# Two mixers of a decoder trunk: float32r parts instead of float32 matmuls, the mask and the pooling sums on VectorE

## The chip, the cores and the metric

One NeuronCore of a Trainium2 chip runs the whole program. The metric is the device time of one execution in microseconds; the reference's outputs are computed in float32 from float32 inputs.

## What is computed

A trunk of two residual layers over 256 positions of width 1024. Each layer is SwiGLU (half step), a mixer, SwiGLU (half step), each behind an RMSNorm whose shift, scale and gate come from a conditioning vector. The even layer's mixer is causal pooling beside differential attention; the odd layer's is an mLSTM. What the change touches:

```python
def pool_mixer(u, w_group, scale):
    ...
    for g, w in enumerate(POOL_WINDOWS):                  # 2, 4, 8, 16
        csg = cs[:, :, g]                                 # cumulative sum over positions
        cs_pad = jnp.pad(csg, ((0, 0), (w, 0), (0, 0)))
        total = cs_pad[:, w:] - cs_pad[:, :S]
        count = jnp.minimum(pos + 1, w).astype(jnp.float32)
        means.append(total / count[None, :, None])
    pooled = jnp.stack(means, axis=2) - ug
    y = jnp.einsum('bsgc,gcd->bsgd', pooled, w_group.astype(jnp.float32))
    ...
def diff_attention(q, k, v, lam_params, subln_g, lambda_init):
    ...
        s = jnp.einsum('bqhcd,bkhcd->bhcqk', qblk, kf)
        s = jnp.where(key_pos[None, :] <= qpos[:, None], s, -jnp.inf)
        p = jax.nn.softmax(s, axis=-1)
        a = p[:, :, 0] - lam * p[:, :, 1]
...
def mlstm_chunkwise(q, k, v, i_pre, f_pre):
    ...
    m_t = jnp.maximum(inter_log, jnp.max(D, axis=-1))
    Dw = jnp.exp(D - m_t[..., None])
```

## The kernel before

Activations lie with features on the 128 partitions and the 256 positions along the free axis. Every weight matrix is cut into units of 128x128; `weight_units` lists them in the order in which they are used, and the host packs them so, 16 units to a DMA. `split_to` makes two float32r parts of each half chunk (8 units): ACT writes the high part `wh` (L297), DVE the low part `wl` (L298). `mm3` then takes a unit with three matmuls (L339 to L341): high by high, low by high, high by low. `unit` counts units, and 8 of them make a block of 128 output rows.

The rest of a mixer runs in generators, the lanes: `tick` goes through them at every unit, and a lane's `yield n` puts off its next piece by n units. `run_until` drives all lanes on at once where the result of one is needed. The compiler's scheduler orders each engine's instructions afterwards, so pieces move by a few matmuls.

Even mixer: `in_proj` computes 16 blocks in the order `EVEN_IN_ORDER` (q, k, v of each of four heads, then u3 to u0). DVE takes each out of PSUM (`ti`, L587), `done` keeps it (ACT, `keep`, L597) and starts lanes. `head` computes the scores of its two halves, on partitions 0 to 63 and 64 to 127: a float32r matmul of an identity with the mask (L624), then float32 matmuls into the same accumulation, 128 columns for the first 128 positions (L626), 256 for the others (L628). DVE takes the row maximum (L635), ACT the exponentials (L639). `pool_group` multiplies u with the group's `w_pool` (L694) and the result with a band matrix that holds mean minus identity (L699 to L701), all in float32; `split_y` (L571, L572) makes the parts of a result for the out projection. That runs over the eight results `ys` in the order `EVEN_OUT_K`, three output blocks side by side at first (`sweep(..., 3, 2)`), and `residual` adds each block to x and prepares the next norm (L436, L383, L384).

Odd mixer: `gates` forms per head the row of running maxima `mr` on 4 partitions and spreads it over 128 with a float32 matmul (L806), one per head, a yield of 6 between them.

`constants` builds masks and band matrices on POOL during the first FFN, in which DVE also sums the conditioning's products (`mod_sums`, L265); that work goes on through most of the run.

## Time and profile before

| | before |
|---|---|
| median of 3 runs | 1001.04 us (1000.83 to 1001.37) |
| profiled execution | 1001.05 us |
| its span, first to last instruction | 999.3 us |
| mean granted TensorE clock | 0.996 |
| PE busy | 980.7 us, 98% |
| DVE busy | 780.8 us, 78% |
| ACT busy | 523.5 us, 52% |
| POOL busy | 209.4 us, 21% |

Busy times are shares of the whole span, and the stages differ. Records of neighbouring instructions on PE overlap (a matmul's record is 0.28 us long and the next one starts 0.12 us later), so the distance of starts tells more than a record's length. A float32 matmul leaves two records, a float32r one or a transpose one. The even mixer runs from about 217 to 306 us, the odd one from about 690 to 800.

### The profile page before, as it was taken

What the parts mean: (1) busy time and instruction counts of PE and PEld (TensorE: products, weight loads), DVE (VectorE), ACT (ScalarE), POOL (GpSimd) and SP (SyncE); (2) the same over time, 40 slices, a digit from 0 to 9 for tenths busy, and PEclk for the clock granted to TensorE, in tenths of its full rate; (3) what the DMA queues carried; (4) which work ended last, traced back from release to release, by engine and by line L of the source; (5) the groups of instructions that cost most, each with busy time, mean ns of one, the idle gap of its engine ahead of it and who ended that gap; (6) DMA issues with size and microseconds to landing.
All of it is one profiled execution on the core that took longest, in us unless ns stands there. A gap on an engine that the chain in (4) does not pass through costs nothing.

```text
span 999.3 us, 19657 instructions
## 1 busy us (share of the span) xinstructions
PE 980.7 (98%) x8032; PEld 965.4 (97%) x8032; DVE 780.8 (78%) x1251; ACT 523.5 (52%) x832; POOL 209.4 (21%) x223
## 2 busy tenths in 40 slices
PE   7999999999999999999999999999999999999996
PEld 6899999998999999999999999999999999999996
DVE  5979998988879888877788888787768987777452
ACT  3475444446765545544454555444667655455441
POOL 4953220110012222211122222000010122222011
PEclk9999999999999999999999999999999999999998
DMA  8978888877647766766766766777546665554521
GB/s 341 318 293 320 328 328 319 343 287 261 216 157 262 257 251 251 258 258 243 285 228 246 264 250 250 268 283 288 212 173 216 255 237 214 205 217 176 187 103 43
DMA packets 36093, 247.18 MB, mean 247 GB/s; under 512 B 4001, under 2 KB 4385, under 8 KB 7458
## 3 DMA queue, kind: packets, MB, share of 16 engines
q1 hardware_dynamic: 35856, 245.81, 66.8%
q8 instruction: 63, 1.03, 0.4%
q14 instruction: 28, 0.23, 0.1%
q10 hardware_dynamic: 146, 0.11, 0.0%
HBM read 244.86 MB, written 1.05 MB: 246 GB/s over the span
## 4 chain that ended last, share of the span: by engine, by line
PE 79%; DVE 11%; ACT 4%; issue 4%; POOL 1%; DVEq 0%; ACTq 0%; POOLq 0%
PE one L339 26%; PE one L341 26%; PE one L340 25%; DVE wl L298 4%; DVE rawm L265 3%; ACT wh L297 2%; DVE xl L384 1%; POOL hr L393 1%; PE one L410 0%; DVE xa L436 0%; DVE acol L360 0%; DVE xl L557 0%; PE one L628 0%; DVE ti L587 0%; PE one L626 0%
## 5 line engine op out<-in xcount | busy, mean ns | idle before, releaser
L339 PE MATMUL one<-xh,wh 128*128 128x258 f32 (+1 forms) x1728 | 486.1, 286 | 1.9 <-ACT xh L555 1.9
L340 PE MATMUL one<-xh,wl 128*128 128x258 f32 (+1 forms) x1728 | 482.2, 283 | 2.1 <-DVE wl L298 2.0
L297 ACT ACTIVATE wh<-raww 128x1024 fp32r<-128x1024 f32 x320 | 337.9, 1058 | 277.2 <-PE one L341 247.5
L341 PE MATMUL one<-xl,wh 128*128 128x258 f32 (+1 forms) x1728 | 481.7, 283 | 0.2
L298 DVE TENSOR_TENSOR wl<-raww,wh 128x1024 fp32r<-128x1024 f32 x320 | 394.9, 1236 | 107.5 <-ACT wh L297 102.4
L339 PEld LDWEIGHTS one<-xh,wh 128*128 128x128 f32 x1728 | 325.7, 190 | 5.3 <-ACT xh L555 2.4
L340 PEld LDWEIGHTS one<-xh,wl 128*128 128x128 f32 x1728 | 326.0, 190 | 4.3 <-DVE wl L298 4.0
L341 PEld LDWEIGHTS one<-xl,wh 128*128 128x128 f32 x1728 | 322.7, 189 | 0.9 <-DVE xl L384 0.6
L339 PE MATMUL one<-hid,wh 128*128 128x256 f32 x832 | 233.8, 281 | 0.2 <-ACT hid L571 0.2
L341 PE MATMUL one<-hid,wh 128*128 128x256 f32 x832 | 233.7, 281 | 0.0
L340 PE MATMUL one<-hid,wl 128*128 128x256 f32 x832 | 233.3, 280 | 0.0
L468 POOL TENSOR_TENSOR hid<-h,hid 128x256 fp32r<-128x256 f32 x88 | 116.2, 1322 | 349.6 <-ACT hid L467 344.0
L339 PEld LDWEIGHTS one<-hid,wh 128*128 128x128 f32 x832 | 156.7, 188 | 0.4 <-ACT hid L571 0.4
L340 PEld LDWEIGHTS one<-hid,wl 128*128 128x128 f32 x832 | 156.8, 188 | 0.0
L341 PEld LDWEIGHTS one<-hid,wh 128*128 128x128 f32 x832 | 156.5, 188 | 0.2 <-DVE hid L572 0.2
L265 DVE CUSTOM_DVE_ANT_0 rawm<-rawm,cact,pk 128x1024 f32<-128x1024 f32 x112 | 150.5, 1370 | 0.0
L377 POOL TENSOR_TENSOR acc<-acc,sq 128x256 f32<-128x256 f32 x41 | 34.4, 839 | 272.0 <-ACT sq L373 271.8
L482 DVE TENSOR_TENSOR t<-one,rext 128x258 f32<-128x258 f32 x132 | 55.3, 422 | 31.1 <-PE one L341 30.2
L463 ACT ACTIVATE sg<-t 128x256 f32<-128x256 f32 x66 | 32.8, 500 | 33.7 <-DVE t L482 33.7
L467 ACT ACTIVATE hid<-h 128x256 fp32r<-128x256 f32 x88 | 36.8, 418 | 19.1 <-DVE h L465 18.7
L265 DVE CUSTOM_DVE_ANT_0 rawm<-rawm,cact,ghalf 128x1024 f32<-128x1024 f32 x32 | 44.8, 1428 | 0.0
L465 DVE SCALAR_TENSOR_TENSOR h<-t,sg 128x256 f32<-128x256 f32 x66 | 32.5, 492 | 8.4 <-ACT sg L463 0.6
(213 smaller groups left out, 503.7 us busy)
## 6 DMA issues: line engine op xcount, KB each, us to landing
raww<-wst SPq DMA_DIRECT2D x152, 1024.0 KB, 4.9
rawm<-mst SPq DMA_DIRECT2D x71, 1024.0 KB, 4.8
raww<-wst SPq DMA_DIRECT2D x16, 512.0 KB, 5.4
xa<-xT SPq DMA_DIRECT2D x2, 512.0 KB, 4.7
rawm<-mst SPq DMA_DIRECT2D x2, 512.0 KB, 7.2
outT<-fin SPq DMA_DIRECT2D x3, 256.0 KB, 2.8
pk<-pack SPq DMA_DIRECT2D x1, 416.0 KB, 6.3
outT<-fin SPq DMA_DIRECT2D x2, 128.0 KB, 2.3
```

The lines of the kernel that those rows point to most:

```text
L265: nc.vector.tensor_tensor_reduce(out=ri, in0=ri, in1=cact, scale=factor, scalar=first, op0=ALU.mult, op1=ALU.add, accum_out=modc[n // KT][ ...
L297: nc.scalar.activation(whs[i], src, AF.Copy)
L298: ins = nc.vector.tensor_tensor(out=wls[i], in0=src, in1=whs[i].bitcast(F32), op=ALU.subtract)
L339: nc.tensor.matmul(out, lhsT=wh, rhs=rh, start=start, stop=False, skip_group_check=skip)
L340: nc.tensor.matmul(out, lhsT=wl, rhs=rh, start=False, stop=False, skip_group_check=skip)
L341: nc.tensor.matmul(out, lhsT=wh, rhs=rl, start=False, stop=stop, skip_group_check=skip)
L377: eng.tensor_tensor(out=stat["acc"], in0=stat["acc"], in1=sq, op=ALU.add)
L463: nc.scalar.activation(sg, gate, AF.Silu, bias=bias_g)
L465: nc.vector.scalar_tensor_tensor(out=h, in0=up, scalar=bias_u, in1=sg, op0=ALU.add, op1=ALU.mult)
L467: nc.scalar.activation(hh[:, 0:T], h, AF.Copy)
L468: nc.gpsimd.tensor_tensor(out=hl[:, 0:T], in0=h, in1=hh[:, 0:T].bitcast(F32), op=ALU.subtract)
L482: nc.vector.tensor_tensor(out=t[:, i, :], in0=ts.pop((f, i))[:, 0:XC], in1=rext, op=ALU.mult)
```

## The change

- **Scores.** q and k are kept as two float32r parts (ACT the high, DVE the low one). A head's scores are twelve float32r matmuls instead of two mask matmuls and four float32 ones: for each of the two column ranges high by high, low by high, high by low, alternating between the halves on partitions 0 to 63 and 64 to 127. The mask is added by DVE in the operation that takes the maximum; it writes the masked scores to SBUF, from where ACT takes the exponentials. The lane waits 10 units instead of 8.
- **Pooling.** The sums over 2, 4, 8, 16 positions come first, by shifted additions on DVE, doubling each time; mean minus token goes into two float32r parts, and three matmuls of 256 columns with the parts of `w_pool` (made once on POOL) follow. The band matrices are gone; `icnt` holds 1/(t+1) for the first 16 positions.
- **Out projection.** `EVEN_OUT_K` takes the last head last, and four blocks run side by side at first, the last three of the eight results late; the host's packing follows.
- **Odd mixer.** `mr` is split into two float32r parts; each row is spread by two float32r matmuls.

```diff
-EVEN_OUT_K = (4, 5, 6, 3, 2, 7, 1, 0)
+EVEN_OUT_K = (4, 5, 6, 3, 2, 1, 0, 7)
+PAD = 16
...
         def head(h):
-            yield 8
+            yield 10
...
-            for c in range(2):
-                rows = slice(64 * c, 64 * c + 64)
-                nc.tensor.matmul(pp[c][:, 0:3 * P], lhsT=identr, rhs=masks3, start=True, stop=False,
-                                 skip_group_check=True)
-                nc.tensor.matmul(pp[c][:, 0:P], lhsT=q[rows, 0:P], rhs=kk[rows, 0:P], start=False, stop=True,
-                                 skip_group_check=True)
-                nc.tensor.matmul(pp[c][:, P:3 * P], lhsT=q[rows, P:T], rhs=kk[rows, 0:T], start=False, stop=True,
-                                 skip_group_check=True)
+            for to, qs, ks in ((slice(0, P), slice(0, P), slice(0, P)), (slice(P, 3 * P), slice(P, T), slice(0, T))):
+                for j, (a, b) in enumerate(((0, 0), (1, 0), (0, 1))):
+                    for c in range(2):
+                        rows = slice(64 * c, 64 * c + 64)
+                        nc.tensor.matmul(pp[c][:, to], lhsT=q[a][rows, qs], rhs=kk[b][rows, ks], start=j == 0,
+                                         stop=j == 2, skip_group_check=True)
...
-                    nc.vector.tensor_reduce(out=mx[:, i, c:c + 1], in_=pp[c][:, cols[i]], axis=AX.X, op=ALU.max)
+                    nc.vector.tensor_tensor_reduce(
+                        out=sc[:, c, cols[i]], in0=pp[c][:, cols[i]], in1=masks3[:, cols[i]], scale=1.0, scalar=NEG,
+                        op0=ALU.add, op1=ALU.max, accum_out=mx[:, i, c:c + 1])
...
         def pool_group(g, src, bias):
...
+            s, d = u, 1
+            while d < w:
+                n = tmp.tile([P, PAD + T], F32, tag="ps", name=nm("ps"))
+                lo = 2 * d - 1
+                nc.vector.tensor_tensor(out=n[:, lo:PAD + T], in0=s[:, lo:PAD + T], in1=s[:, lo - d:PAD + T - d],
+                                        op=ALU.add)
+                s, d = n, 2 * d
             z = slot()
...
+            nc.vector.scalar_tensor_tensor(out=z[:, 0:T], in0=s[:, PAD:PAD + T], scalar=1.0 / w,
+                                           in1=u[:, PAD:PAD + T], op0=ALU.mult, op1=ALU.subtract)
+            e = z[:, 0:w - 1]
+            nc.vector.tensor_tensor(out=e, in0=s[:, PAD:PAD + w - 1], in1=icnt[:, 0:w - 1], op=ALU.mult)
+            nc.vector.tensor_tensor(out=e, in0=e, in1=u[:, PAD:PAD + w - 1], op=ALU.subtract)
+            zh, zl = slot(F32R), slot(F32R)
+            nc.scalar.activation(zh[:, 0:T], z[:, 0:T], AF.Copy)
+            nc.vector.tensor_tensor(out=zl[:, 0:T], in0=z[:, 0:T], in1=zh[:, 0:T].bitcast(F32), op=ALU.subtract)
+            yield 14
...
+            for j, (a, b) in enumerate(((wph, zh), (wpl, zh), (wph, zl))):
+                nc.tensor.matmul(ps[:, 0:T], lhsT=a[:, sl], rhs=b[:, 0:T], start=j == 0, stop=j == 2)
...
+            ph, pl = slot(F32R), slot(F32R)
+            nc.scalar.activation(ph[:, 0:T], src, AF.Identity, bias=bias)
+            nc.vector.scalar_tensor_tensor(out=pl[:, 0:T], in0=src, scalar=bias, in1=ph[:, 0:T].bitcast(F32),
+                                           op0=ALU.add, op1=ALU.subtract)
+            parts[blk] = (ph, pl)
...
-        to_x(l, 1, sweep(range(KT), EVEN_OUT_K, 3, 2), EVEN_OUT_K, rhs, nxt)
+        to_x(l, 1, sweep(range(KT), EVEN_OUT_K, 4, 3), EVEN_OUT_K, rhs, nxt)
...
+            nc.vector.tensor_copy(mrs[0], mr)
+            nc.vector.tensor_tensor(out=mrs[1], in0=mr, in1=mrs[0].bitcast(F32), op=ALU.subtract)
...
-                nc.tensor.matmul(pb4[:, 0:T], lhsT=ident[0:4, h:h + 1].broadcast_to([4, P]), rhs=mr,
-                                 start=True, stop=True)
+                for j in range(2):
+                    nc.tensor.matmul(pb4[:, 0:T], lhsT=identr[0:4, h:h + 1].broadcast_to([4, P]), rhs=mrs[j],
+                                     start=j == 0, stop=j == 1)
```

How the built program's rows move, at three places. The line numbers of the new program differ: its weight matmuls are L334 to L336, the head's L621, the pool's L709, the odd rows' L824; on DVE `wl` is L293, `ti` L582, the conditioning's sums L260.

PE, the first head's scores, before:

```order
L341 MATMUL one_2764<-xl_96,wh_2674 128x258
L624 MATMUL one_2789<-masks_122,identr 128x384
L626 MATMUL one_2789<-hid_2746,hid_2742 128x128
L628 MATMUL one_2789<-hid_2746,hid_2742 128x256
L624 MATMUL one_2790<-masks_122,identr 128x384
L626 MATMUL one_2790<-hid_2746,hid_2742 128x128
L628 MATMUL one_2790<-hid_2746,hid_2742 128x256
L339 MATMUL one_2764<-xh_89,wh_2674 128x258
L340 MATMUL one_2764<-xh_89,wl_2675 128x258
```

and in the changed kernel:

```order
L336 MATMUL one_2732<-xl_98,wh_2638 128x258
L621 MATMUL one_2778<-hid_2712,hid_2706 128x128
L621 MATMUL one_2779<-hid_2712,hid_2706 128x128
L621 MATMUL one_2778<-hid_2712,hid_2707 128x128
L621 MATMUL one_2779<-hid_2712,hid_2707 128x128
L334 MATMUL one_2769<-xh_83,wh_2678 128x258
L335 MATMUL one_2769<-xh_83,wl_2679 128x258
L336 MATMUL one_2769<-xl_91,wh_2678 128x258
L621 MATMUL one_2778<-hid_2713,hid_2706 128x128
L621 MATMUL one_2779<-hid_2713,hid_2706 128x128
L621 MATMUL one_2778<-hid_2712,hid_2706 128x256
L621 MATMUL one_2779<-hid_2712,hid_2706 128x256
```

The mask matmuls are gone, the two accumulators (`one_2778`, `one_2779`) alternate, and the twelve matmuls of the first head stand in two pieces with three weight matmuls between them. Those of the other three heads stand in one piece, each between weight matmuls.

DVE, from the last head's softmax to the blocks u2 and u1, before:

```order
L643 TENSOR_SCALAR r_496_3264<-rs_3253,lamc_2640 128x2
L298 TENSOR_TENSOR wl_3357<-raww_3354,wh_3356 128x1024
L646 SCALAR_TENSOR_TENSOR sc_3249<-sc_3249,r_496_3264 128x128
L646 SCALAR_TENSOR_TENSOR sc_3249<-sc_3249,r_496_3264 128x256
L587 TENSOR_TENSOR ti_3347<-one_3311,rext 128x258
L298 TENSOR_TENSOR wl_3404<-raww_3354,wh_3403 128x1024
L391 TENSOR_SCALAR hv_3368<-ss_3364 128x2
L265 ISA rawm_3352,mod_110<-rawm_3352,cact,pk 128x1024
L265 ISA mod_110 128x1
L587 TENSOR_TENSOR ti_3398<-one_3351,rext 128x258
```

and in the changed kernel (`pu` is u behind 16 zero columns, `ps` its sums):

```order
L638 TENSOR_SCALAR r_504_3274<-rs_3263,lamc_2604 128x2
L693 TENSOR_TENSOR ps_3316<-pu_3313 128x271
L641 SCALAR_TENSOR_TENSOR sc_3259<-sc_3259,r_504_3274 128x128
L641 SCALAR_TENSOR_TENSOR sc_3259<-sc_3259,r_504_3274 128x256
L693 TENSOR_TENSOR ps_3318<-ps_3316 128x269
L582 TENSOR_TENSOR ti_3368<-one_3332,rext 128x258
L693 TENSOR_TENSOR ps_3320<-ps_3318 128x265
L293 TENSOR_TENSOR wl_3393<-raww_3390,wh_3392 128x1024
L693 TENSOR_TENSOR ps_3322<-ps_3320 128x257
L293 TENSOR_TENSOR wl_3461<-raww_3390,wh_3460 128x1024
L697 SCALAR_TENSOR_TENSOR hid_3324<-ps_3322,pu_3313 128x256
L693 TENSOR_TENSOR ps_3373<-pu_3370 128x271
```

The group of 16 positions has its four additions between the softmax's operations, an evacuation and two `wl`; the other groups follow in the same manner among the next three `wl`.

PE, the first broadcast row of the odd mixer, before:

```order
L341 MATMUL one_8924<-xl_97,wh_8836 128x258
L791 MATMUL one_8954<-dg_1397_8896,ones 128x8
L794 MATMUL one_8954<-ident,mr_8889 128x4 x2
L806 MATMUL one_8967<-mr_8889,ident 128x256
L339 MATMUL one_8924<-xh_90,wh_8836 128x258
L340 MATMUL one_8924<-xh_90,wl_8837 128x258
```

and in the changed kernel:

```order
L336 MATMUL one_8964<-xl_97,wh_8876 128x258
L805 MATMUL one_8994<-dg_1419_8936,ones 128x8
L808 MATMUL one_8994<-ident,mr_8929 128x4 x2
L824 MATMUL one_9011<-mrh_9007,identr 128x256
L334 MATMUL one_8964<-xh_90,wh_8876 128x258
L824 MATMUL one_9011<-mrl_9008,identr 128x256
L335 MATMUL one_8964<-xh_90,wl_8877 128x258
```

The low part's matmul of the first row stands behind one weight matmul; in the other three rows the two parts follow each other.

## Rows read from the trace of the kernel before

**Rows 1.** The page, part 1: busy us (share of the span) and instructions of each engine.

```profile
PE 980.7 (98%) x8032; PEld 965.4 (97%) x8032; DVE 780.8 (78%) x1251; ACT 523.5 (52%) x832; POOL 209.4 (21%) x223
```

**Rows 2.** Waits of PE, whole run: waiter, releaser, us in total, times, longest.

```profile
PE one L340 <- DVE wl L298: 2.0, 7, 0.4
```

**Rows 3.** Timeline of PE, a head's scores: start us, us, engine, line, operation.

```profile
233.39 0.28 PE L341 MATMUL one<-xl,wh 128*128 128x258 f32 x1
233.51 0.34 PE L624 MATMUL one<-masks,identr 128*128 128x384 f32 x1
233.78 0.49 PE L626 MATMUL one<-hid,hid 64*128 64x128 f32 x2
234.11 0.59 PE L628 MATMUL one<-hid,hid 64*128 64x256 f32 x2
234.63 0.44 PE L624 MATMUL one<-masks,identr 128*128 128x384 f32 x1
...
236.07 0.28 PE L340 MATMUL one<-xh,wl 128*128 128x258 f32 x1
```

**Rows 4.** Timeline of PE, a pool group's projection, then two groups' band matmuls.

```profile
270.77 0.28 PE L341 MATMUL one<-xl,wh 128*128 128x258 f32 x1
270.88 0.60 PE L694 MATMUL one<-pk,hid 128*128 128x128 f32 x4
...
271.45 0.28 PE L340 MATMUL one<-xh,wl 128*128 128x258 f32 x1
...
281.00 0.39 PE L699 MATMUL one<-band,hid 128*128 128x128 f32 x2
...
281.67 0.39 PE L699 MATMUL one<-band,hid 128*128 128x128 f32 x2
```

**Rows 5.** Timeline of PE, a broadcast row of the odd mixer.

```profile
718.67 0.29 PE L341 MATMUL one<-xl,wh 128*128 128x258 f32 x1
718.89 0.69 PE L806 MATMUL one<-mr,ident 4*128 4x256 f32 x2
...
719.74 0.28 PE L340 MATMUL one<-xh,wl 128*128 128x258 f32 x1
719.86 0.28 PE L341 MATMUL one<-xl,wh 128*128 128x258 f32 x1
```

**Rows 6.** Windows, the even mixer: us, busy time of each engine, clock, DMA share, GB/s.

```profile
216.84:311.20 94.36, 94.04 (x746) 89.14 (x745) 76.69 (x157) 61.10 (x143) 10.94 (x13) 1.00 0.61 221
```

**Rows 7.** Waits of DVE in 216.84 to 311.2 us.

```profile
DVE wl L298 <- ACT wh L297: 6.8, 8, 1.6
DVE ti L587 <- PE one L341: 3.7, 4, 2.1
DVE hid L572 <- ACT hid L571: 3.1, 6, 1.2
```

**Rows 8.** Timeline of DVE: an evacuation and the next; three residuals and the next.

```profile
271.57 0.42 DVE L587 TENSOR_TENSOR ti<-one,rext 128x258 f32<-128x258 f32 x1
271.91 1.27 DVE L265 CUSTOM_DVE_ANT_0 rawm<-rawm,cact,pk 128x1024 f32<-128x1024 f32 x1
...
288.69 1.26 DVE L436 SCALAR_TENSOR_TENSOR xa<-one,mod,xa 128x256 f32<-128x256 f32 x3
289.87 1.07 DVE L384 SCALAR_TENSOR_TENSOR xl<-xa,acol,xh 128x256 fp32r<-128x256 f32 x2
```

**Rows 9.** Timeline of DVE, the first FFN's steps: every second `wl`.

```profile
39.10 1.52 DVE L298 TENSOR_TENSOR wl<-raww,wh 128x1024 fp32r<-128x1024 f32 x1 [0.30 <-ACT wh L297]
...
45.57 1.28 DVE L298 TENSOR_TENSOR wl<-raww,wh 128x1024 fp32r<-128x1024 f32 x1 [0.55 <-ACT wh L297]
...
58.01 1.28 DVE L298 TENSOR_TENSOR wl<-raww,wh 128x1024 fp32r<-128x1024 f32 x1 [0.55 <-ACT wh L297]
...
64.01 1.23 DVE L298 TENSOR_TENSOR wl<-raww,wh 128x1024 fp32r<-128x1024 f32 x1 [0.53 <-ACT wh L297]
```

**Rows 10.** Windows, the first FFN's start.

```profile
26.84:64.01 37.17, 35.79 (x288) 34.49 (x287) 33.94 (x48) 17.95 (x25) 32.87 (x66) 1.00 0.96 346
```

More of the change, by code (lines that the diff above doesn't have):

```diff
@@ L101, in weight_units @@
                 units += [(("in_even", l // 2), k, EVEN_OFF[a] + i) for (a, i), k in sweep(EVEN_IN_ORDER, range(KT))]
-                units += [(("out_even", l // 2), k, n) for n, k in sweep(range(KT), EVEN_OUT_K, 3, 2)]
+                units += [(("out_even", l // 2), k, n) for n, k in sweep(range(KT), EVEN_OUT_K, 4, 3)]
             else:
@@ L177, in trunk_kernel @@
     modc = [const.tile([P, KT], F32, name=f"mod{g}") for g in range(DEPTH * NSUB * 3)]
-    masks3 = const.tile([P, 3 * P], F32R, name="masks3")
+    masks3 = const.tile([P, 3 * P], F32, name="masks3")
     identr = const.tile([P, P], F32R, name="identr")
@@ L181, in trunk_kernel @@
     tri = const.tile([P, P], F32, name="tri")
-    band = const.tile([P, len(WINDOWS), 3 * P], F32, name="band")
+    icnt = const.tile([P, PAD], F32, name="icnt")
+    wph = const.tile([P, 512], F32R, name="wph")
+    wpl = const.tile([P, 512], F32R, name="wpl")
     wgh = const.tile([P, 64], F32R, name="wgh")
@@ L219, in constants @@
                                 fill=0.0, base=0, channel_multiplier=-1)
[L220 to L230 removed]
+        for t in range(PAD):
+            nc.gpsimd.memset(icnt[:, t:t + 1], 1.0 / (t + 1))
         nc.sync.dma_start(pk2, pack2)
@@ L233, in constants @@
         nc.gpsimd.tensor_tensor(out=wgl, in0=pcol("w_gates", 0, 64), in1=wgh.bitcast(F32), op=ALU.subtract)
+        nc.gpsimd.tensor_copy(wph, pcol("w_pool", 0, 512))
+        nc.gpsimd.tensor_tensor(out=wpl, in0=pcol("w_pool", 0, 512), in1=wph.bitcast(F32), op=ALU.subtract)
     mod_sched = mod_schedule(nchunks)
@@ L638, in head @@
                 for c in range(2):
-                    nc.scalar.activation(sc[:, c, cols[i]], pp[c][:, cols[i]], AF.Exp, bias=nb[:, i, c:c + 1],
+                    nc.scalar.activation(sc[:, c, cols[i]], sc[:, c, cols[i]], AF.Exp, bias=nb[:, i, c:c + 1],
                                          scale=0.125, accum_out=sm[:, i, c:c + 1])
@@ L688, in pool_group @@
         def pool_group(g, src, bias):
-            u = keep(src, bias)
-            yield 16
-            pz = one()
-            for i in range(2):
-                sl = slice(i * P, (i + 1) * P)
-                nc.tensor.matmul(pz[:, sl], lhsT=u[:, sl], rhs=pcol("w_pool", g * P, P), start=True, stop=True)
-            z = slot()
-            nc.scalar.activation(z[:, 0:T], pz[:, 0:T], AF.Copy)
-            yield 18
+            w = WINDOWS[g]
+            u = tmp.tile([P, PAD + T], F32, tag="pu", name=nm("pu"))
+            nc.vector.memset(u[:, 0:PAD], 0.0)
+            nc.scalar.activation(u[:, PAD:PAD + T], src, AF.Identity, bias=bias)
+            s, d = u, 1
[5 more added lines that the diff above has]
+                s, d = n, 2 * d
+            z = slot()
+            nc.vector.scalar_tensor_tensor(out=z[:, 0:T], in0=s[:, PAD:PAD + T], scalar=1.0 / w,
[7 more added lines that the diff above has]
+            yield 14
             ps = one()
-            nc.tensor.matmul(ps[:, 0:P], lhsT=z[:, 0:P], rhs=band[:, g, 0:P], start=True, stop=True)
-            nc.tensor.matmul(ps[:, P:T], lhsT=z[:, 0:P], rhs=band[:, g, P:T], start=True, stop=False)
-            nc.tensor.matmul(ps[:, P:T], lhsT=z[:, P:T], rhs=band[:, g, T:3 * P], start=False, stop=True)
+            sl = slice(g * P, (g + 1) * P)
+            for j, (a, b) in enumerate(((wph, zh), (wpl, zh), (wph, zl))):
+                nc.tensor.matmul(ps[:, 0:T], lhsT=a[:, sl], rhs=b[:, 0:T], start=j == 0, stop=j == 2)
             ys[g] = split_y(ps[:, 0:T], pcol("pool_scale", g))
@@ L708, in done @@
                 return
-            parts[blk] = keep(src, bias)
             if kind == "v":
+                parts[blk] = keep(src, bias)
                 spawn(turn_v(i))
+                return
+            ph, pl = slot(F32R), slot(F32R)
[3 more added lines that the diff above has]
+            parts[blk] = (ph, pl)
             if kind == "k":
```

19 lines of the change are left out of this document (4 added, 15 removed).

## Prediction

> **What bounds the kernel now.** I read the page first: TensorE (PE) is busy 980.7 of 999.3 us [rows 1]. Then its waits: behind the first 70 us it hardly waits for anybody (the largest sum shown behind the start is 2.0 us in seven waits for a weight's low part) [rows 2]. So a PE instruction removed is time gained, as long as nobody else becomes late. What a PE instruction costs can't be read from its recorded length, since neighbours overlap; I read it from start to start. One weight matmul costs 0.12 us (719.74 to 719.86 [rows 5]); 7680 of them are 922 us. Everything else on PE is laid between them, and its price is the distance from the matmul before it to the second one behind it, less 0.24.
>
> - Scores of a head: 233.39 to 236.07, less 0.24: **2.44 us** [rows 3], four times.
> - A pool group: its projection 270.77 to 271.45 less 0.24 = **0.44**, its three band matmuls 281.00 to 281.67 = **0.67** [rows 4], four times.
> - A broadcast row in the odd mixer: 718.67 to 719.74 less 0.24 = **0.83** [rows 5], four times.
>
> What float32 costs is in the same rows: a 128-column float32 matmul is two records of 0.11 each, a 256-column one twice that (0.44). So 0.83 holds 0.39 that is no streaming. A head's 2.44 holds 2x0.18 for the masks (384 columns at the rate of 0.12 for 256), 2x0.22 and 2x0.44 for the scores: 1.68, and 0.76 over. Operands on 64 or 4 partitions stand between operands on 128, once (two edges) for a row, twice (four edges) for a head: both give 0.19 per edge. The Trainium skill (TensorEngine Tiling, Key Properties) says that changing the tiling mode drains the engine; the 0.39 and 0.76 agree with it.
>
> **The change, part by part.**
>
> *Pool matmuls.* Three 256-column float32r matmuls on 128 partitions, the shape of the weight matmuls, replace 1.11 us: 3x0.12 = 0.36, so 0.75 less, four times: **-3.0**. This is the best founded term.
>
> *Scores.* Twelve float32r matmuls on 64 partitions, six of 256 columns and six of 128. 256 columns: 0.12. No row shows a float32r matmul under 256 columns. Bounds: half of 0.12 (0.06) below, the float32 matmul of that shape (0.22) above. I take 0.11, one record of a 128x128 pass with its own weight load [rows 4]. With two edges: 0.38 + 6x0.12 + 6x0.11 = 1.76, so 0.68 less, four times -2.72. By the order, the first head stands in two pieces with a weight block between: two more edges, +0.39. **-2.3**.
>
> *Odd rows.* 0.39 + 2x0.12 = 0.63 instead of 0.83: -0.2, four times -0.8; the first row is torn apart by one weight matmul: two more edges, +0.39. **-0.4**. The two 4x256 DVE operations that make the parts (under 0.4 each) stand ahead of a yield of 14 units, about 5 us in which that lane waits anyway: nothing.
>
> *DVE.* The low parts of q and k are eight operations with a column scalar, 0.39 each (288.69 to 289.87 for three [rows 8]): 3.2. The sums are 10 additions, four scaled subtractions and four low parts, 0.34 each (271.57 to 271.91 [rows 8]): 6.1; eight corrections of the first columns at 0.07 to 0.2 and the memsets: 0.6. The mask's addition rides on the maximum that was there; I cost it at the same, at most 0.1 more for each of 16. Sum **9.9 us**. Between 216.84 and 311.20 DVE works 76.69 of 94.36 us, so it idles 17.7 [rows 6]. PE will need 5.3 us less there, 89.0; DVE needs 86.6, and keeps 2.4 us of idle time. Of today's 17.7, the waits for a high part of the weights (6.8) and for PE's blocks (3.7) [rows 7] come from being ahead, and go when DVE is not ahead. 7.2 are left; 3.1 of them are the waits of the split at L572, in the stretch into which the sums move. So 4.1 us must fit into 2.4: PE waits **+1.7**; bounds 0 (all shrink) and 4.8 (none of the 7.2 does). The wait would be seen in the last input blocks, at the pool matmuls and at `ys`, and again behind the out projection, where four residuals instead of three now come at once. ACT's exponentials read another memory and its pool copy makes a high part instead: nothing, it is busy 61 of 94 us [rows 6].
>
> The Trainium skill (VectorE: DVE Perf Modes, The DRAIN you can't avoid) says that the next DVE operation starts only when the pipe of the one before is empty. By it each of the 26 large additions would cost its whole 0.42 to 0.48, 2.2 us more in all; rows 8 show the next starting 0.08 before the recorded end.
>
> *Constants.* POOL loses the band matrices and gains 16 one-column memsets and the two parts of `w_pool`. It was busy 32.9 of the 37.2 us in which the first FFN starts [rows 10], a stretch paced by DVE: a step took 6.47 (39.10 to 45.57) and 6.22 (45.57 to 58.01, two steps) beside POOL's work and 6.00 (58.01 to 64.01) with little of it [rows 9]. Three steps are 0.9 over; the parts of `w_pool` still fall there. **-0.6**, bounds 0 and -0.9.
>
> *Order of the out projection.* It moves no work on PE: four blocks go side by side instead of three, the last head is wanted after 28 units instead of five. SP's issues keep their order.
>
> **Sum:** -3.0 - 2.3 - 0.4 + 1.7 - 0.6 = -4.6. The profiled execution took 1001.05 (span 999.3), the median of the runs is 1001.04, so both lead to **996.4 us**.
>
> **Rivals.**
>
> A is the forecast, its own range 994.5 to 998.5 by the bounds above.
>
> B, *both halves of a head at once*: the twelve matmuls alternate between partitions 0 to 63 and 64 to 127, and two run in the time of one. A head is 0.38 + 3x0.12 + 3x0.11 = 1.07, the scores -5.1 in all; DVE then has 86.3 us for 86.6, and PE waits 4.4. Between 992.0 (no wait) and 996.3, say 994. The Trainium skill (TensorEngine Tiling, Key Properties) says that different tiles work in parallel. No row here has both halves side by side, which is why it isn't the forecast.
>
> C, *narrow float32r at float32's price*: 0.22 for 128 columns. A head is 0.38 + 0.72 + 1.32 = 2.42, nothing gained and 0.4 lost on the split head; DVE has room and PE doesn't wait. -3.0 + 0.3 - 0.4 - 0.6: 997.4. For it: all float32r rows have 256 columns or more.
>
> D, *loads that don't hide on 64 partitions*: from L626 to L628 it is 0.33 where 128 partitions take 0.22 [rows 3]. If that 0.11 is a weight load and not an edge, twelve matmuls pay it: 3.08 a head, scores +3.0, total 1000.0.
>
> E, *slower: DVE sets the pace*. The waits for the high parts don't shrink, because these in turn wait for PE's buffers; then 14.0 us of idle must fit into 2.4 between 216.84 and 311.20, and PE waits 11.6: 1006.3. It decides the sign once more than 8.7 us of today's 17.7 stay. Against it: DVE would then be behind, and ACT ahead of it.
>
> F, *every DVE operation waits for the one before to empty*: 2.2 us more on DVE, as much more on PE: 998.6. This is the skill's page on DVE above; rows 8 speak against it.
>
> **How the numbers follow.** Chances: A 0.44, B 0.14, C 0.22, D 0.09, E 0.08, F 0.03. A measurement of this kernel can tell about 0.2%, 2 us, from no change. Faster than 999.0: A 0.40, B 0.13, C 0.17, F 0.02 = 0.72. Within: A 0.03, B 0.01, C 0.05, D 0.08, E 0.01, F 0.01 = 0.19. Slower: A 0.01, D 0.01, E 0.07 = 0.09. The range reaches from the middle of B to a little above D, 993.0 to 1000.5; E, the fast half of B and the tail of D stay out, under 0.2.
>
> **What would show it.** Right: a pool group three starts 0.12 apart; a head of 1.7 to 1.8 us by the same measure; DVE over 95% busy from 216 to 306, with PE waits of 1 to 3 us there; first steps near 6.0. B: a head near 1.1 us. C: 0.22 between the narrow matmuls. D: 0.2 between all twelve. E: PE's waits for `wl` and `ys` above 6 us. I am wrong if PE's time outside the even mixer moves by over a microsecond other than in the first 66 us.

## The result, and the profile after

The changed kernel is slower by 0.6%: 1007.06 us median (1005.37 to 1007.43) against 1000.93 (1000.56 to 1001.37) of the kernel before on the same chip, a ratio of 1.0059 [1.0046, 1.0071]. The forecast was 996.4, range 993.0 to 1000.5. The profiled execution took 1006.83 us, its span is 1005.1 (999.3 before).

The page of the changed kernel, busy time of each engine:

```profile
PE 976.7 (97%) x8012; PEld 964.4 (96%) x8012; DVE 790.0 (79%) x1307; ACT 524.0 (52%) x832; POOL 187.5 (19%) x186
```

PE is busy 4.0 us less than in [rows 1] though the span grew by 5.8; DVE's 790.0 are 9.2 more, about what was forecast.

Windows of the changed kernel (columns as in [rows 6]): the stage, two stretches of 20 us, and two short stretches:

```profile
216.30:317.30 101.00, 90.75 (x727) 88.01 (x726) 86.10 (x210) 61.85 (x143) 11.34 (x13) 0.93 0.57 199
250.00:270.00 20.00, 16.76 (x140) 15.81 (x138) 18.89 (x45) 14.78 (x38) 0.69 (x1) 0.98 0.64 219
270.00:290.00 20.00, 13.95 (x81) 13.67 (x82) 14.39 (x53) 8.41 (x24) 1.59 (x1) 0.68 0.46 158
271.10:275.80 4.70, 4.67 (x21) 4.67 (x22) 3.75 (x9) 0.64 (x2) 0.00 (x0) 0.50 0.60 218
281.70:286.00 4.30, 4.30 (x20) 4.22 (x21) 2.78 (x20) 1.67 (x5) 0.00 (x0) 0.50 0.68 236
```

The loss lies in 270 to 290: PE busy 13.95 of 20 at a mean clock of 0.68. DVE idles 14.9 of 101 us over the stage, so it isn't full; but in the 20 us before, it works 18.89.

Waits of PE in 200 to 320 us (columns as in [rows 2]):

```profile
PE one L669 <- ACT hid L664: 4.9, 1, 4.9
PE one L709 <- ACT hid L703: 4.0, 1, 4.0
PE one L621 <- DVE hid L723: 0.6, 2, 0.3
PE one L336 <- DVE xl L379: 0.5, 1, 0.5
```

Two waits hold almost all of it, one each: L709, the first pool group's matmuls, and L669, the transposes of the third head's output (the last head's come at 293.8 and wait for nobody). Timeline of PE: a head, the two waits, a later pool group:

```profile
244.23 0.28 PE L336 MATMUL one<-xl,wh 128*128 128x258 f32 x1
244.44 1.04 PE L621 MATMUL one<-hid,hid 64*128 64x128 f32 x12
245.40 0.39 PE L334 MATMUL one<-xh,wh 128*128 128x258 f32 x1
245.63 0.28 PE L335 MATMUL one<-xh,wl 128*128 128x258 f32 x1
...
266.81 0.28 PE L336 MATMUL one<-xl,wh 128*128 128x258 f32 x1
271.13 0.58 PE L709 MATMUL one<-hid,wph 128*128 128x256 f32 x1 [4.04 <-ACT hid L703]
...
276.44 0.28 PE L336 MATMUL one<-xl,wh 128*128 128x258 f32 x1
...
281.65 0.73 PE L669 MATMUL one<-ident,hid 128*128 128x128 f32 x2 [4.92 <-ACT hid L664]
...
290.63 0.28 PE L709 MATMUL one<-hid,wph 128*128 128x256 f32 x1
290.75 0.28 PE L709 MATMUL one<-hid,wpl 128*128 128x256 f32 x1
290.87 0.28 PE L709 MATMUL one<-hid,wph 128*128 128x256 f32 x1
290.99 0.28 PE L334 MATMUL one<-hid,wh 128*128 128x256 f32 x1
```

By the measure of [rows 3] a head takes 245.63 - 244.23 - 0.24 = 1.16 us instead of 2.44, and a pool group's three are 0.12 apart. From start to start the waits cost 4.32 and 5.20, less 0.12 each: 9.3. Behind each, 19 or 20 starts, transposes among them, stand 0.215 apart instead of 0.12 at clock 0.50, the 1.2 GHz level: 1.8 and 1.9, together 3.7.

What the first wait waits for: DVE, from the evacuation of block u3 to its last correction, the rows of the chain and the long ones between:

```profile
261.67 0.42 DVE L582 TENSOR_TENSOR ti<-one,rext 128x258 f32<-128x258 f32 x1
262.01 1.27 DVE L260 CUSTOM_DVE_ANT_0 rawm<-rawm,cact,pk 128x1024 f32<-128x1024 f32 x1
...
263.40 1.25 DVE L260 CUSTOM_DVE_ANT_0 rawm<-rawm,cact,pk 128x1024 f32<-128x1024 f32 x1
...
264.71 0.43 DVE L693 TENSOR_TENSOR ps<-pu 128x271 f32<-128x271 f32 x1
...
266.75 1.21 DVE L293 TENSOR_TENSOR wl<-raww,wh 128x1024 fp32r<-128x1024 f32 x1
...
268.22 1.21 DVE L293 TENSOR_TENSOR wl<-raww,wh 128x1024 fp32r<-128x1024 f32 x1
269.36 0.41 DVE L697 SCALAR_TENSOR_TENSOR hid<-ps,pu 128x256 f32<-128x256 f32 x1
...
270.47 0.16 DVE L701 TENSOR_TENSOR hid<-hid,pu 128x15 f32<-128x15 f32 x1
```

The chain's own DVE work is some 1.9 us (four additions and L697 at 0.34, the corrections). It takes from 261.67 to 270.6, since two sums of the conditioning and two `wl` for later weights stand between. One link is ACT's: its copy `pu`, from 263.18 to 263.68, without which the first addition can't start. PE reaches the place 14 units after the block, at 266.9.

ACT in the same time; [2.48 <- DVE] is idle time and what ended it:

```profile
270.66 0.42 ACT L703 ACTIVATE hid<-hid 128x256 fp32r<-128x256 f32 x1 [2.48 <-DVE hid L701]
...
276.76 1.06 ACT L292 ACTIVATE wh<-raww 128x1024 fp32r<-128x1024 f32 x1 [5.02 <-PE one L336]
277.72 0.40 ACT L703 ACTIVATE hid<-hid 128x256 fp32r<-128x256 f32 x1
...
278.43 0.25 ACT L660 ACTIVATE hid<-one 128x128 f32<-128x128 f32 x1
...
281.23 0.62 ACT L664 ACTIVATE hid<-one,hr 128x128 f32<-128x128 f32 x2 [1.83 <-POOL hr L388]
```

L660, the squares of the third head's output, has had its input since PE's L655 at about 264.9. In ACT's queue it stands behind L703, which waits for the sums above, and behind a `wh`, which waits 5.02 us for PE to release a buffer. So it runs at 278.43, and PE waits for L664 until 281.65.

PE releases that buffer with the matmul at 276.44, the last one ahead of its own wait (276.44 + 0.28 = 276.72). From there the steps follow one another while PE stands: `wh`, the next L703, a copy of u, the squares, a small DVE step (`hv`, L386, at 279.36), a power on POOL (`hr`, L388, at 279.60) and L664. So PE waits for work that ACT's order lets start only when PE has come to its wait. The chain has a link in DVE's queue too.

### The profile page after: what moved, and what is told of

It is laid out like the page before. It is cut to its first block, busy times and chain, and to the rows that moved or that the text cites. A ratio compares the mean times of both kernels' runs of the same rounds, so it can differ in the third digit from the quotient of the medians.

```text
span 1005.1 us, 19637 instructions
## 1 busy us (share of the span) xinstructions
PE 976.7 (97%) x8012; PEld 964.4 (96%) x8012; DVE 790.0 (79%) x1307; ACT 524.0 (52%) x832; POOL 187.5 (19%) x186
## 4 chain that ended last, share of the span: by engine, by line
PE 76%; DVE 13%; ACT 5%; issue 4%; POOL 1%; DVEq 0%; ACTq 0%; POOLq 0%
PE one L336 25%; PE one L334 25%; PE one L335 25%; DVE wl L293 5%; DVE rawm L260 4%; ACT wh L292 2%; DVE xl L379 1%; POOL hr L388 1%; DVE ti L582 1%; PE one L405 0%; DVE acol L355 0%; ACT sc L634 0%; DVE xa L431 0%; DVE xl L552 0%; DVE sc L628 0%
## 5 line engine op out<-in xcount | busy, mean ns | idle before, releaser
L334 PE MATMUL one<-xh,wh 128*128 128x258 f32 (+1 forms) x1728 | 486.9, 286 | 2.1 <-ACT xh L550 2.1
L336 PE MATMUL one<-xl,wh 128*128 128x258 f32 (+1 forms) x1728 | 482.7, 284 | 0.8 <-DVE xl L379 0.8
L293 DVE TENSOR_TENSOR wl<-raww,wh 128x1024 fp32r<-128x1024 f32 x320 | 393.7, 1233 | 105.3 <-ACT wh L292 100.2
L334 PEld LDWEIGHTS one<-xh,wh 128*128 128x128 f32 x1728 | 326.8, 191 | 3.7 <-ACT xh L550 2.6
L336 PEld LDWEIGHTS one<-xl,wh 128*128 128x128 f32 x1728 | 323.9, 189 | 1.4 <-DVE xl L379 1.2
L334 PE MATMUL one<-hid,wh 128*128 128x256 f32 x832 | 234.2, 282 | 0.0
L336 PE MATMUL one<-hid,wh 128*128 128x256 f32 x832 | 234.1, 281 | 0.0
L334 PEld LDWEIGHTS one<-hid,wh 128*128 128x128 f32 x832 | 157.4, 189 | 0.0
L336 PEld LDWEIGHTS one<-hid,wh 128*128 128x128 f32 x832 | 157.1, 189 | 0.0
L260 DVE CUSTOM_DVE_ANT_0 rawm<-rawm,cact,pk 128x1024 f32<-128x1024 f32 x112 | 150.2, 1366 | 0.0
L260 DVE CUSTOM_DVE_ANT_0 rawm<-rawm,cact,ghalf 128x1024 f32<-128x1024 f32 x32 | 44.7, 1428 | 0.0
```

Source lines behind the costliest of these rows:

```text
L260: nc.vector.tensor_tensor_reduce(out=ri, in0=ri, in1=cact, scale=factor, scalar=first, op0=ALU.mult, op1=ALU.add, accum_out=modc[n // KT][ ...
L293: ins = nc.vector.tensor_tensor(out=wls[i], in0=src, in1=whs[i].bitcast(F32), op=ALU.subtract)
L334: nc.tensor.matmul(out, lhsT=wh, rhs=rh, start=start, stop=False, skip_group_check=skip)
L336: nc.tensor.matmul(out, lhsT=wh, rhs=rl, start=False, stop=stop, skip_group_check=skip)
```

## Experiments

The theory after the result (called *backlog* in the first expectations): PE's work fell as forecast, and the loss is two chains that arrive late through DVE's and ACT's queues, with half clock behind. Rivals: the loss is tied to the place of PE's wait; to the half clock; or DVE as a whole is short of time.

**Parts alone.** e3 and e4 put one part each into the kernel before: the diff's pieces *Scores*, or *Pooling* and *Out projection* with the constants.

> The kernel before, with the scores' part of the change alone (q and k in two parts, twelve matmuls, mask added by DVE); pooling, out projection's order and odd rows as before. By the trace of the changed kernel the four heads cost 5.98 us instead of 9.78, waits of 0.6 for the low parts included: 996.8 to 997.6 if nothing else waits. Rival (the 3.2 us of low parts and the longer maximum are already too much for DVE): waits at PE of 2 us or more, 999 or above.

> The kernel before, with the pooling's part and the out projection's new order alone (sums on DVE, no band matrices, less on POOL at the start); scores and odd rows as before. Its PE work is 3.0 us less and the start 0.6 shorter. Backlog: DVE has some 4 us less queued than in the changed kernel, so the waits shrink from 9.0 to 4 to 6, with half clock behind one of them: 1001 to 1004. Rival (the pooling by itself fits, only both parts together are too much): 997.0 to 998.0.

The scores alone: 998.55, ratio 0.9978 [0.9969, 0.9988], 1 us above what was expected. By the places of the same weight matmuls its profiled execution is 0.56 later than the kernel before at 71 us, gains 3.5 at the scores, and gives back 1.0 between 269 and 319 us. The pool part alone: 1004.69, ratio 1.0037 [1.0023, 1.0051], slower by itself, and 0.7 above what backlog gave. Waits of PE in e4, 200 to 320 us:

```profile
PE one L710 <- ACT hid L704: 4.3, 1, 4.3
PE one L670 <- ACT hid L665: 0.7, 1, 0.7
```

The first wait comes with the pool part alone; the second is 0.7 here, 0.7 in e3 too, and 4.9 with both. Against the kernel before in the same sessions the parts' sum is -2.3 + 3.8 = 1.5; together, with the odd rows, they cost 6.1.

**The place of the wait.** e1: pool matmuls later.

```diff
             nc.vector.tensor_tensor(out=zl[:, 0:T], in0=z[:, 0:T], in1=zh[:, 0:T].bitcast(F32), op=ALU.subtract)
-            yield 14
+            yield 18
```

> The changed kernel, with the yield ahead of the pool matmuls 18 units instead of 14; nothing else. By the built order the first pool group's matmuls stand eight units (2.9 us) later on PE, the others two to four. Theory 'place' (the matmuls only stand too early for a chain that is otherwise on time): the first wait of 4.0 us falls to about 1, the half clock behind it goes, the second wait of 4.9 us, which was only passed on, shrinks with it: 994 to 998. Theory 'backlog' (DVE has more queued work between 251 and 275 than it can do there, and the transposes of head 2 hang on the same queue through ACT): the wait moves from the pool matmuls to the transposes, which can start only some 2 us earlier than now: 1003.5 to 1005.5.

1003.9, ratio 1.0031 [1.0019, 1.0043]: backlog held. Waits of PE:

```profile
PE one L669 <- ACT hid L664: 5.8, 1, 5.8
PE one L709 <- ACT hid L703: 1.2, 1, 1.2
PE one L709 <- DVE hid L704: 0.9, 1, 0.9
```

Of the first wait 2.1 is left, and the second grew by 0.9.

**Less work on DVE ahead of the chain.** e2 shortens four of the conditioning's sums to 8 columns; e7 gives the ten additions to POOL; e10 issues the conditioning's sums earlier, so that none runs between 258 and 305 us.

```diff
+                ri, ca = (ri[:, 0:8], cact[:, 0:8]) if m in (30, 31) else (ri, cact)
                 nc.vector.tensor_tensor_reduce(
-                    out=ri, in0=ri, in1=cact, scale=factor, scalar=first,
+                    out=ri, in0=ri, in1=ca, scale=factor, scalar=first,
...
-                nc.vector.tensor_tensor(out=n[:, lo:PAD + T], in0=s[:, lo:PAD + T], in1=s[:, lo - d:PAD + T - d],
+                nc.gpsimd.tensor_tensor(out=n[:, lo:PAD + T], in0=s[:, lo:PAD + T], in1=s[:, lo - d:PAD + T - d],
...
-MOD_POINTS = ((8, 8), (41, 32), (72, 44), (104, 56), (124, 68), (145, 72))
+MOD_POINTS = ((8, 8), (33, 27), (39, 32), (42, 32), (72, 44), (104, 56), (124, 68), (145, 72))
```

> The changed kernel, but four of the conditioning's sums on DVE (1.2 us each, at 262.0, 263.4, 270.9 and 272.8) read 8 columns instead of 1024: their results are left out of the computation, the transfers stay. It takes 2.4 us of DVE work from ahead of the first pool group's parts and 4.8 from ahead of the second's. Backlog: first wait 4.0 to about 1.6, the transposes come about 4.8 us earlier, less half clock: 999.5 to 1002.5. Rival (hops between engines set the wait, not queued work): under 1 us gained, 1006 to 1007.

> The changed kernel, with the ten shifted additions of the pooling on POOL instead of DVE. DVE has 1.4 us less ahead of the first pool group's parts and 2.4 less ahead of the second's; POOL's additions take 0.8 to 1.3 each by its rows, four in a chain for the first group. Backlog: both waits shrink by 1 to 3 us: 1001 to 1005. Rival (the chain's hops set the wait, and POOL's are longer): 1007.5 or more.

> The changed kernel, with the schedule of the conditioning's transfers steeper from weight chunk 33 to 39 and flat from 39 to 42, so that the four sums that fall between 262 and 274 us run before 252 us. Nothing is left out. Backlog: DVE has 4.8 us less ahead of the second pool group's parts, as in e2: first wait under 2.7, 1001 to 1004. Rival (DVE has no room earlier either, and the heads become late): new waits of over 1 us at scores or transposes before 262 us, 1005 or more.

e2: 1003.91, ratio 1.0021 [1.0011, 1.0031]; its runs reach from 1001.01 to 1004.06, so its size is loose. The waits are 2.7 and 3.7. The direction is backlog's, the size smaller: the median lies between the two ranges. Two of the shortened sums take 2.4 us out ahead of the first group, but its first addition starts only 1.0 earlier (263.70 instead of 264.71), when ACT's `pu` ends; DVE stands idle 0.9 there. e10: 1003.9, ratio 1.003 [1.0018, 1.0042], inside backlog's range: the first wait is 1.5, the second 3.7, but the scores now wait 1.8 for their parts. e7: 1006.81, ratio 1.006 [1.0045, 1.0075], no gain, which neither theory had. DVE in e7:

```profile
265.57 1.43 DVE L641 SCALAR_TENSOR_TENSOR sc<-sc,r 128x128 f32<-128x128 f32 x2
267.62 0.42 DVE L697 SCALAR_TENSOR_TENSOR hid<-ps,pu 128x256 f32<-128x256 f32 x1 [0.62 <-POOL ps L693]
267.96 1.66 DVE L293 TENSOR_TENSOR wl<-raww,wh 128x1024 fp32r<-128x1024 f32 x1
269.55 0.16 DVE L700 TENSOR_TENSOR hid<-ps,icnt 128x15 f32<-128x15 f32 x1
269.63 1.21 DVE L293 TENSOR_TENSOR wl<-raww,wh 128x1024 fp32r<-128x1024 f32 x1
270.76 0.60 DVE L701 TENSOR_TENSOR hid<-hid,pu 128x15 f32<-128x15 f32 x1
```

L697 runs 1.7 us earlier than before the edit, yet the two corrections behind it still stand behind a `wl` each and end no earlier; DVE's own operations take longer beside POOL (1.43 instead of 0.74 for L641, 1.66 instead of 1.21 for the first `wl`; the second takes 1.21 as before, though POOL adds beside it too). The Trainium skill (GPSIMD Engine Reference, Specifications) names contention of GpSimd with DVE instructions that have two SBUF inputs; L641 and the first `wl` agree. So busy time removed from DVE gained nothing here, by the corrections' place in its queue and by the slower operations; the run doesn't part the two.

**The half clock.** e5 gives PE 32 matmuls to do in the first wait, whose results aren't used.

```diff
+            for j in range(32 if g == 3 else 0):
+                nc.tensor.matmul(ps[:, 0:T], lhsT=wph[:, sl], rhs=wpl[:, 0:T], start=True, stop=True)
```

> The changed kernel, with 32 more matmuls (256 columns, 128 partitions, on constants, overwritten by the group's own start) ahead of the first pool group's; 32 x 0.12 = 3.8 us, about the wait of 4.0. They compute nothing that is used. Theory (half clock follows the wait): PE works through the wait, its clock stays at the upper level from 271 to 276, where 18 matmuls took 0.215 instead of 0.12: 1.7 to 2.0 us less, unless the second wait takes it back: 1004.8 to 1005.5 or, taken back, 1006.5 to 1007. In either case the granted clock between the two waits reads 1.00. Rival (the half clock has another cause): it stays, 1007 or above.

1005.14, ratio 1.0041 [1.0026, 1.0056]: 1.9 below the changed kernel, as expected. Windows of e5 behind the first wait and behind the second:

```profile
271.00:276.50 5.50, 3.70 (x29) 3.31 (x27) 5.50 (x16) 2.83 (x5) 0.00 (x0) 1.00 0.75 289
281.00:286.00 5.00, 5.00 (x27) 5.00 (x26) 2.54 (x12) 1.71 (x4) 0.00 (x0) 0.53 0.38 162
```

Where PE worked through most of its wait (1.1 us of it is left), the clock stays 1.00 and the starts stand 0.12 apart; behind the second wait, through which PE idles for 4.3 us, it is 0.53. The half clock follows the wait, and this one was worth some 1.9.

**The head.** e6 is e3 with all six matmuls of half 0 ahead of those of half 1.

```diff
-            for to, qs, ks in ((slice(0, P), slice(0, P), slice(0, P)), (slice(P, 3 * P), slice(P, T), slice(0, T))):
-                for j, (a, b) in enumerate(((0, 0), (1, 0), (0, 1))):
-                    for c in range(2):
-                        rows = slice(64 * c, 64 * c + 64)
+            for c in range(2):
+                rows = slice(64 * c, 64 * c + 64)
+                for to, qs, ks in ((slice(0, P), slice(0, P), slice(0, P)), (slice(P, 3 * P), slice(P, T), slice(0, T))):
+                    for j, (a, b) in enumerate(((0, 0), (1, 0), (0, 1))):
```

> The kernel with the scores' part alone (998.55), but all six matmuls of a head's first half ahead of the six of its second. Theory (the two halves run at the same time when they alternate): a head goes from 1.16 to about 1.65 to 1.8 us, four times: 1000.4 to 1001.2. Rival (the matmuls are short in any order): 998.3 to 998.9.

A miss, between the two ranges: 999.13, ratio 0.9983 [0.9974, 0.9993]. Timeline of PE in e6:

```profile
245.54 0.28 PE L340 MATMUL one<-xl,wh 128*128 128x258 f32 x1
245.75 1.23 PE L625 MATMUL one<-hid,hid 64*128 64x128 f32 x12
...
247.14 0.28 PE L339 MATMUL one<-xh,wl 128*128 128x258 f32 x1
```

A head is 247.14 - 245.54 - 0.24 = 1.36, only 0.2 more than alternating. In the built program all six matmuls of the first half stand ahead of those of the second, yet from the first half's third on the two run side by side (starts at 246.028 and 246.035). In the changed kernel the pairs start 0.003 to 0.004 apart. So both halves at once is shown; this edit doesn't put them in a strict sequence.

**Curing the second wait.** e9 is e1 with the pool's high part made by DVE, so that ACT's queue no longer waits for the sums. e8 computes u0 first and u3 last, uses the eight results one by one over the first four output blocks, in the order 4, 5, 6, 0, 1, 2, 3, 7, and waits longer (pool 18, transposes 16). e11 takes e9, e10, u0 first, and the results one by one in the order below; e13 is e11 without e10's edit.

```diff
-            nc.scalar.activation(zh[:, 0:T], z[:, 0:T], AF.Copy)
+            nc.vector.tensor_copy(zh[:, 0:T], z[:, 0:T])
...
-EVEN_IN_ORDER = _blocks("q0 k0 v0 q1 k1 v1 q2 k2 v2 q3 k3 v3 u3 u2 u1 u0")
+EVEN_IN_ORDER = _blocks("q0 k0 v0 q1 k1 v1 q2 k2 v2 q3 k3 v3 u0 u1 u2 u3")
...
-EVEN_OUT_K = (4, 5, 6, 3, 2, 1, 0, 7)
+EVEN_OUT_K = (4, 5, 0, 6, 1, 2, 3, 7)
...
-        to_x(l, 1, sweep(range(KT), EVEN_OUT_K, 4, 3), EVEN_OUT_K, rhs, nxt)
+        to_x(l, 1, sweep(range(KT), EVEN_OUT_K, 4, 8), EVEN_OUT_K, rhs, nxt)
```

> The changed kernel with four edits for the backlog: u0 first (one addition) and u3 last (four); the out projection takes them in that order and goes result by result over its first four blocks, so that the first pooled result is wanted 12 units after the input blocks instead of 3; the pool matmuls wait 18 units instead of 14, the last transposes of a head 16 instead of 12. No work is taken away. Backlog that can be laid beside other PE work: waits at the pool matmuls and transposes of 2 us or less, clock 1.00 throughout; PE's work gives 1000.9 - 0.6 - 3.8 - 3.0 - 0.4 = 993.2, with 1 to 2 us of other waits 994 to 996. Rival (DVE is short over the whole stage): the waits come back at the weights' low parts or at the results, 6 us or more: 1000 or above.

> The kernel of e1_pool_later (1003.9), with the high part of the pooled values made by DVE instead of ACT; DVE gets four operations of 0.34 us more, ACT four of 0.32 less. In e1 ACT stood twice for 2.5 us at that operation, with the squares of head 2, whose input had been there for 10 us, queued behind it. Theory (ACT's order passes DVE's lateness on to the transposes): the wait of 5.8 us at the transposes shrinks to 3 to 4: 1001 to 1002.5. Rival (DVE's own queue sets the transposes): no gain or a loss by the 0.34s: 1003.5 to 1004.5.

> The changed kernel with the edits together: conditioning's sums earlier (as e10), high part of the pooled values on DVE (as e9), u0 first and u3 last, pool matmuls after 18 units, out projection result by result over four blocks in the order 4, 5, 0, 6, 1, 2, 3, 7. No computation is left out and no work is taken away. If order and queue places made the loss: PE's waits between 216 and 300 us sum to 2 us or less, its clock stays at 1.00, 993 to 996. Rival (VectorE lacks the time in this stage): waits of 5 us or more come back elsewhere, 999 or above.

> The kernel of e11_all_four (1002.95) without the earlier conditioning sums; the rest as there. It is the base for e14. The waits at the scores before 262 us, which the earlier sums had brought, go (about 2.5 us); DVE has 4.8 us more between 262 and 274. If VectorE's load sets the transposes of head 2, their wait is 6 us or more: 1003 to 1005; if ACT's order does, it stays at 4 to 4.5: 1000 to 1002.

e8: 1005.38, ratio 1.0046 [1.0031, 1.0061], a miss, in the rival's range: the transposes wait 3.9, a weight matmul of the out projection 2.4. e9: 1004.88, ratio 1.0037 [1.0024, 1.005]: a loss of 1.0 against e1, the rival's direction and 0.4 above its range; the transposes wait 6.8, since the squares end at 273.2 and DVE's `hv` comes only at 276.80. e11: 1002.95, ratio 1.0019 [1.001, 1.0029], far above what was expected and in its rival's range: the pool's wait is gone, the transposes still wait 4.5, the scores 1.8. e13: 1003.41, ratio 1.0024 [1.0014, 1.0033], transposes 4.7: by its time VectorE's load, by its wait rather ACT's order, so e13 doesn't decide. In all four a wait for L664 stayed, whichever way DVE's work was moved. ACT in e13:

```profile
269.61 0.51 ACT L688 ACTIVATE pu<-ti 128x256 f32<-128x256 f32 x1 [0.96 <-DVE ti L582]
271.81 1.06 ACT L292 ACTIVATE wh<-raww 128x1024 fp32r<-128x1024 f32 x1 [1.70 <-PE one L336]
272.77 0.26 ACT L660 ACTIVATE hid<-one 128x128 f32<-128x128 f32 x1
```

Now the squares, whose input is there at 265.1, stand behind a `pu` that waits for DVE and a `wh` that waits for PE. So e14 changes the order on ACT: it is e13 with the next `wh` and the next `pu` issued behind the squares of the latest head, here the third (this moves the line numbers by five or six; the transposes are L674, the pool's matmuls L715). e15 is e11 with the same order, e16 the changed kernel with this order and the high part on DVE, e17 is e15 with the head's yield 13 instead of 10.

```diff
-            nc.scalar.activation(whs[i], src, AF.Copy)
+            if last_sq[0] is None:
+                nc.scalar.activation(whs[i], src, AF.Copy)
+            else:
+                with tc.issue_after(last_sq[0].ins):
+                    nc.scalar.activation(whs[i], src, AF.Copy)
...
-                nc.scalar.activation(oq[:, sl], po[:, sl], AF.Square, accum_out=ss[:, i:i + 1])
+                last_sq[0] = nc.scalar.activation(oq[:, sl], po[:, sl], AF.Square, accum_out=ss[:, i:i + 1])
...
-            nc.scalar.activation(u[:, PAD:PAD + T], src, AF.Identity, bias=bias)
+            with (tc.issue_after(last_sq[0].ins) if last_sq[0] else nullcontext()):
+                nc.scalar.activation(u[:, PAD:PAD + T], src, AF.Identity, bias=bias)
```

> e13 with one edit in the order of ACT: the next high parts of the weights and the next copies of u are issued behind the squares of the last head; no work is added or left out. In e11 the squares had their input at 268.1 us and stood behind two high parts that waited for PE until 274.5. If ACT's order sets the transposes: their wait falls to 1 us or less, the clock stays at 1.00, and the time falls by 4 to 6 us against e13: 995 to 998. If VectorE's load sets them: less than 1.5 us against e13.

> e11_all_four with the same edit in the order of ACT. The wait of 4.2 us at the transposes goes, with half clock behind it; the waits at the scores before 262 us (2.5 us) stay: 997 to 999. If VectorE's load sets the transposes: no more than 1.5 us under e11, 1001.5 or above.

> The changed kernel with ACT's order alone edited: the high part of the pooled values on DVE (as e9) and the squares of a head ahead of the next high parts of the weights and copies of u (as e14); places of the pool matmuls, order of the groups and of the out projection as in the changed kernel. ACT's order as the cause of the second wait: the first wait stays at 3.5 to 4.5 us with half clock behind it, the second of 4.9 falls under 1.5 and its half clock goes: 999.5 to 1001.5. Rival (the first wait passes the second on, whatever ACT does): 1004 or more.

> e15 (998.05) with the yield ahead of a head's scores 13 units instead of 10. In e15 PE waits at the scores for parts of q and k at 225, 235 and 256 us, 2.3 us by the distances of starts. They go, and the first head stands in one piece: 996.0 to 997.2. Rival (the later heads only move the wait to the transposes or to the last result): 997.8 to 998.5.

e14: 999.01, ratio 0.998 [0.997, 0.999], 4.4 below e13, by the edit in ACT's order alone. Timeline of ACT in e14:

```profile
267.50 0.27 ACT L665 ACTIVATE hid<-one 128x128 f32<-128x128 f32 x1
...
272.30 0.62 ACT L669 ACTIVATE hid<-one,hr 128x128 f32<-128x128 f32 x2 [1.73 <-POOL hr L393]
```

The squares come at 267.50 instead of 272.77; behind them `hv` still stands in DVE's queue until 271.30. The windows 270 to 290 of e13 and of e14:

```profile
270.00:290.00 20.00, 14.86 (x97) 13.87 (x96) 16.15 (x52) 7.29 (x20) 2.06 (x2) 0.83 0.48 163
```

```profile
270.00:290.00 20.00, 16.13 (x131) 15.34 (x130) 18.78 (x58) 11.11 (x23) 1.41 (x2) 1.00 0.48 164
```

The clock is 1.00 again. In e14 the pool's matmuls wait 2.2 and a weight matmul of the out projection 1.9, both for DVE, and the total is above the 995 to 998 expected. e15: 998.05, ratio 0.9969 [0.9958, 0.9981], as expected, and no single wait of this stage is longer than 0.8. It leaves out none of VectorE's work, so VectorE isn't short of time over the stage. e17: 998.57, ratio 0.9976 [0.9967, 0.9986]; the waits moved, the rival held. e16: 1002.79, ratio 1.0022 [1.0013, 1.0031], between its two ranges:

```profile
PE one L715 <- DVE hid L709: 6.3, 2, 3.5
...
PE one L674 <- ACT hid L669: 0.2, 1, 0.2
```

With the order and the high part on DVE the transposes wait 0.2 instead of 4.9, and the pool's matmuls 6.3 instead of 4.0: now two groups behind DVE's queue. The squares run at 267.19, but `hv` only at 273.91, and the first pool group's wait of 3.5 gave it that time. So each wait can go while the other stays, and with either left the kernel is slower than the one before (e13 and e16).

**The best version.** e12 is the kernel before with the scores and the odd rows only.

```diff
+            mrs = [small.tile([4, T], F32R, tag=n, name=nm(n), bufs=1) for n in ("mrh", "mrl")]
+            nc.vector.tensor_copy(mrs[0], mr)
+            nc.vector.tensor_tensor(out=mrs[1], in0=mr, in1=mrs[0].bitcast(F32), op=ALU.subtract)
```

> The kernel before with the scores' part and the odd rows' part, pooling as before. From 998.55 (scores alone) less 0.3 to 0.4 for the rows: 998.0 to 998.4. If the split first row costs what the other three gain: 998.5.

997.93 (997.85 to 998.44), ratio 0.9973 [0.9962, 0.9984]: the fastest together with e15, without the pool part.

## Why the prediction was wrong

Positions of the same weight matmul in both profiled executions give each term (their shift, after minus before):

| step | forecast | measured | how |
|---|---|---|---|
| Constants | -0.6 | -0.55 | shift from 66 us on |
| Scores | -2.3 | -3.5 | shift grows from -0.55 to -4.02 at 268.7 us of before, where both have done the same transposes |
| Pool matmuls | -3.0 | -3.0 | three starts 0.12 apart |
| DVE full, PE waits | +1.7 (0 to 4.8) | +13.0 | two waits 9.3, half clock 3.7 |
| Odd rows | -0.4 | -0.4 | shift falls from 6.25 to 5.87 |
| sum | -4.6 | +5.6 | at the end of the weight matmuls |

The measured terms add to 5.55; smaller shifts of both signs (a wait of 0.5 for `xl` among them) nearly cancel.

- *Pool matmuls*, *Odd rows*, *Constants*: right to a tenth. The torn first row cost what it was given.
- *Scores*: the step that priced twelve matmuls in sequence (0.11 and 0.12 each) failed; rival B's mechanism holds. B forecast 1.07 a head; one in one piece that waits for nobody takes 1.16. The torn first head takes 1.84 and the other two 1.44 and 1.54, waits for parts of q and k included (0.34 in the first, 0.24 in the last). The Trainium skill (TensorEngine Tiling (Array Packing), Key Properties) says that different tiles work in parallel: the trace agrees, with starts 0.003 us apart. Rivals C and D are out with it.
- **The failed step is "PE waits +1.7".** DVE's added work was sized right (9.9 forecast, 9.2 measured). What failed is the argument from it: idle time summed over 94 us against work summed over 94 us. It asked whether DVE would get through, and it did, with 14.9 us idle: 75.3 of 89.7 us busy up to 306, 84%, where the forecast wanted over 95%. DVE's waits for the weights' high parts, which were to go, are still 5.7 of the 14.9 (6.8 of 17.7 before). It didn't ask when one result would come through. The forecast even had the order for it: the additions among an evacuation, the softmax's pair and two `wl`, ahead of a yield of 14 units, about 5 us; the conditioning's two sums stand just ahead of the rows shown there. In the trace the chain (1.9), the pair (0.7), two evacuations (0.7), two `wl` (2.3) and the conditioning's two sums (2.6) make 8.2 us. Such a sum against 5 would have shown a first wait of some 3 us; it measured 4.0, and 4.3 in e4.
- The second wait was in no rival: a ready ACT instruction that stands behind others in its queue. The prediction costed ACT at "nothing, it is busy 61 of 94 us", which is true (61.85) and beside the point. e13 and e14 differ in nothing but the edit in this order, and by 4.4 us.
- The half clock behind a wait had no term; e5 shows some 1.9 for one.
- E came near by its number (1006.3), not by its mechanism: DVE doesn't set the pace over the stage, and PE's waits for `wl` aren't among the waits shown. F gets no support: on DVE the next operation still starts before the recorded end of the one before (264.71 + 0.43, and L641 at 265.07 in the trace of the changed kernel). The section that F rests on (the Trainium skill, VectorE: DVE Perf Modes, The DRAIN you can't avoid) itself adds that a next operation which isn't held starts earlier; the prediction left that out.

Shown by experiment: the pool part brings the first wait (e4), its size moves with the place and with what is ahead on DVE (e1, e2, e10), and the second wait goes with ACT's order (e14 against e13; e16, which also moves the high part). Not shown: that ACT's order alone would do in the changed kernel, since `hv` on DVE is a link of the same chain (e9, e16). Only argued: why the scheduler puts the squares so late there. A version with the pool's additions cut out of DVE's queue without slowing DVE wasn't tried.
